# One more product per pair in a seven-product matmul stage, with its operands 0, 64 or 128 bytes apart

## The chip, the cores and the metric

The kernel runs on one core of a Trainium2 chip. The metric is the time of one execution on the device, in microseconds (us), lower being better. A time is the median of the runs shown; a profile is one further execution, and its own time is given beside it.

## The reference

One layer of an encoder over 512 tokens of 1024 channels, all in float32:

```python
h = rms_norm(x, norm1_g)
proj = h @ w_in                       # pooling, attention, recurrence, gates
...                                   # three branches, gated and summed, w_out, residual
h2 = rms_norm(x, norm2_g)
gu = h2 @ w_ffn_in                    # (512, 1024) @ (1024, 2 * 2816)
x = x + (silu(gu[..., :2816]) * gu[..., 2816:]) @ w_ffn_out
return rms_norm(x, final_norm_g)
```

The change lies in the line `gu = h2 @ w_ffn_in`.

## The kernel before

Products of float32 matrices are made from rounded parts: each operand is split into `hi` (rounded to the matmul's float32r form, a cast on ScalarE) and `lo` (the rest, a subtraction on VectorE), and a product is three matmuls into one PSUM bank: hi by hi, hi by lo and lo by hi. `whi` and `wlo` are the parts of weights, `shi` and `slo` those of sums of weights, `h_hi` and `h_lo` those of the transposed activations, `fhi` and `flo` those of sums of activations.

The hidden layer has 22 blocks of 128 gate columns and 22 of 128 up columns. Block 0 is computed plainly. Blocks 1 to 21 are pairs, one gate block and one up block each, of a two by two scheme with seven products in place of eight: the 1024 channels are halved, the 512 tokens are halved, and the products are of sums of halves. One product (`product`, helper `mm`, line 90) is 12 matmuls: three terms of 4 blocks of 128 channels, with 256 tokens (columns) streaming and 128 weight columns standing in the array. A pair is four bodies, `first` (products into `x` and `zy`), `second`, `third` (two each) and `fourth` (one), 84 matmuls in all. `first` uses part 0 of the pair, the split weights of one block (`whi`, 1024 elements per partition); `second` and `third` use parts 1 and 2 (`shi`, `slo`, from `sums`); `fourth` uses part 3 (`whi`, 512 elements).

TensorE works in the order in which the program is written. The other engines' instructions are placed by a scheduler that models the time, each engine working through its own queue in order. What comes between:

- The raw weights of a pair come by two DMAs from the SP queue into one of two `raw` buffers; the next transfer starts when the last reader of a buffer is done.
- Line 180 (ScalarE) and line 181 (VectorE) split parts 0 and 3 into `whi` and `wlo`, of which there are three buffers each; a cast waits until TensorE has read the old contents. Lines 258, 261 and 262 make `sums` on VectorE; lines 297 and 299 split them into `shi` and `slo`.
- Results are taken out of PSUM at lines 1123, 1134, 1136 and 1155 (ScalarE) and 1145, 1150 and 1156 (VectorE), the last of which writes the hidden block.

PSUM has three banks called `mm`, three called `rc` and two called `tp`. In the pairs `x` lies in an `mm` bank and `zy` in an `rc` bank. `tp` is used before the pairs for transposes and after them as the fourth accumulator of the output projection; during the pairs it is free.

Some places of tiles in the built program, in bytes from the start of a partition: the three `whi` buffers 35104, 39200 and 43296, `wlo` 47392, 51488 and 55584, the first norm's activations `hT` 69408 and 85792, `shi` 162080 and 166176, `slo` 170272 and 174368, all 32 past a multiple of 128. `h_hi` (61408), `h_lo` (77792), `fhi` (178656) and `flo` (195040) start 96 past one; `pad` lines of the program shift them. A block of 128 weight columns takes 512 bytes, one of 256 or 512 tokens 1024 or 2048, so that these remainders hold for every block.

Of the kernel before, what the change touches and what calls it, by code (L numbers as in the profile page):

```python
# [18 lines left out]
P = 128  # L19
# [57 lines left out]
def encoder_kernel(ctx: ExitStack, tc: tile.TileContext, x, norm1_g, w_in, pool_w, pool_scale,  # L77
# [11 lines left out]
    def mm(out_, lhsT, rhs, start, stop, chain=False):  # L89
        i = nc.tensor.matmul(out_, lhsT=lhsT, rhs=rhs, start=start, stop=stop, skip_group_check=chain)  # L90
        tc.keep_in_program_order(i)
        n = 1
        for d in rhs.shape[1:]:
            n *= d
        pipe.t += max(0.107, n * 0.0004167 + 0.002) if rhs.dtype == F32R else max(0.216, n * 0.001667 + 0.004)
# [18 lines left out]
    def bank(name, shape=(P, 512)):  # L114
        return psum.tile(list(shape), F32, name=name, bufs=2 if name == "tp" else 3)
# [148 lines left out]
    @contextmanager  # L264
    def behind(after):

        with ExitStack() as st:
            for i in after:
                st.enter_context(tc.issue_after(i))
            yield  # L270
# [45 lines left out]
    def product(ps, part, n, r, start):  # L316

        terms = [(part.hi, r[0]), (part.hi, r[1]), (part.lo, r[0])]
        for i, (w, m) in enumerate(terms):
            for k in range(KT // 2):  # L320
                mm(ps, w[:, n, k, :], m[:, k, :], start and i == 0 and k == 0,
                   i == 2 and k == KT // 2 - 1, True)
                if k % 2:
                    yield
# [147 lines left out]
    for b in range(NB):  # L472
# [3 lines left out]
        if b >= 1:  # L476
            c = OFF[("rq", "rf", "rb")[b - 1]]
# [583 lines left out]
    def ffn_pair_evac(j, pg, pu):  # L1061
        sl = FF["t"].tile([P, S], F32, name="silu")
        nc.scalar.activation(out=sl, in_=pg, func=AF.Silu)
        nc.vector.tensor_tensor(out=hid_of(j), in0=pu, in1=sl, op=ALU.mult)

    def hid_of(j):
        return FF["hid"][j // 8][:, j % 8, :]
# [3 lines left out]
    def hid_split(half, jp):  # L1071

        if (half, jp) in hid_parts:
            return
        early = half == 0 and jp < 2
        hi, lo = ((LAST["ws"] if early else FF["hs"]).tile([P, 2, S], F32R, name=n)
                  for n in (("shi", "slo") if early else ("hhi", "hlo")))
        j = 2 * jp
        view = FF["hid"][j // 8][:, j % 8:j % 8 + 2, :]
        nc.scalar.copy(out=hi, in_=view)  # L1080
        nc.vector.tensor_tensor(out=lo, in0=view, in1=hi.bitcast(F32), op=ALU.subtract)
        hid_parts[half, jp] = hi, lo
# [31 lines left out]
    def ffn_pair_bodies(j):  # L1114
        c = {}


        def first(part):
            f = FF["forms"]
            c["x"], c["zy"] = bank("mm")[:, 0:256], bank("rc")  # L1120
            c["u"] = FF["t"].tile([P, S], F32, name="u")
            yield from product(c["x"], part, 0, f.r11, True)
            nc.scalar.copy(out=c["u"][:, 0:256], in_=c["x"])
            yield from product(c["zy"][:, 0:256], part, 1, f.r21, True)

        def second(part):
            f = FF["forms"]
            y = c["y"] = c["zy"][:, 256:]
            if j == 2:
                with behind(FF["s12_2"]):  # L1130
                    ffn_pair_evac(0, *FF["first"])
            c["g"] = FF["t"].tile([P, S // 2], F32, name="g2")
            yield from product(c["x"], part, 1, f.n2, False)
            nc.scalar.copy(out=c["u"][:, 256:], in_=c["x"])
            yield from product(y, part, 0, f.n1, True)
            FF["y1"] = (nc.scalar.copy(out=c["g"], in_=y).ins,)

        def third(part):
            f = FF["forms"]
            if j == 1:  # L1140
                with behind(FF["forms_end"]):
                    pairs[2][1].chunk.add()
            c["sl"] = FF["t"].tile([P, S], F32, name="silu")
            yield from product(c["x"], part, 0, f.d, False)
            on_dve = nc.vector.tensor_tensor(out=c["g"], in0=c["x"], in1=c["g"], op=ALU.add).ins
            if j == 1:
                FF["g1"] = (on_dve,)
            nc.scalar.activation(out=c["sl"][:, 256:], in_=c["g"], func=AF.Silu, scale=-1.0)
            yield from product(c["y"], part, 1, f.r22, False)
            nc.vector.tensor_tensor(out=c["u"], in0=c["u"], in1=c["zy"], op=ALU.add)  # L1150

        def fourth(part):
            f = FF["forms"]
            yield from product(c["x"], part, 0, f.n4, False)
            nc.scalar.activation(out=c["sl"][:, 0:256], in_=c["x"], func=AF.Silu, scale=-1.0)
            nc.vector.tensor_tensor(out=hid_of(j), in0=c["sl"], in1=c["u"], op=ALU.mult)
            if j == FT - 1:
                for jp in range(2):
                    hid_split(0, jp)

        return first, second, third, fourth

    pair_bodies = {j: ffn_pair_bodies(j) for j in range(1, FT)}
    after = {1: (None, None, "forms_mid", "forms_mid"), 2: ("g1",) * 4, 3: ("s12_2",) * 4}
    pairs = {j: pair_parts(j, *ffn_cols(j), after.get(j, (None,) * 4)) for j in range(1, FT)}
# [71 lines left out]
    for half in range(2):  # L1237
        ps = list(row_parts(w_ffn_out[0], 0, FT, half * 512))
        n = NPC if half == 0 else NPC - TAIL
# [126 lines left out]
```

## Time and profile before

| | |
|---|---|
| runs | 912.06, 912.14 and 913.32 us; median 912.14 us |
| profiled execution | 912.07 us, of which the span of the profile is 910.3 us |
| TensorE matmuls, weight loads | 887.8 us busy (5353), 782.5 us (5353) |
| VectorE, ScalarE, GpSimd | 582.2, 420.9 and 62.0 us busy |
| DMA | 89.01 MB, on average 98 GB/s |

A line of the profile's timeline has the start and the length of a group of like instructions in us, the engine (PE is TensorE's matmuls, PEld its weight loads, DVE VectorE, ACT ScalarE, POOL GpSimd, SP the queue of the DMAs), the source line, the operation, "output<-inputs" by the program's names, the size, how many there are, and in brackets how long the engine had idled and what it had waited for. Matmuls overlap, so that the step from one start to the next, not the length, tells what one costs in a row of them.

### The profile page before, as it was taken

What the parts mean: (1) busy time and instruction counts of PE and PEld (TensorE: products, weight loads), DVE (VectorE), ACT (ScalarE), POOL (GpSimd) and SP (SyncE); (2) the same over time, 40 slices, a digit from 0 to 9 for tenths busy, and PEclk for the clock granted to TensorE, in tenths of its full rate; (3) what the DMA queues carried; (4) which work ended last, traced back from release to release, by engine and by line L of the source; (5) the groups of instructions that cost most, each with busy time, mean ns of one, the idle gap of its engine ahead of it and who ended that gap; (6) DMA issues with size and microseconds to landing.
All of it is one profiled execution on the core that took longest, in us unless ns stands there. A gap on an engine that the chain in (4) does not pass through costs nothing.

```text
span 910.3 us, 13173 instructions
## 1 busy us (share of the span) xinstructions
PE 887.8 (98%) x5353; PEld 782.5 (86%) x5353; DVE 582.2 (64%) x876; ACT 420.9 (46%) x652; POOL 62.0 (7%) x62
## 2 busy tenths in 40 slices
PE   6999999999999999999999999999999999999996
PEld 5977987887898888778888898999999999888885
DVE  5696553663867865654325554998888888644544
ACT  5544423433655674332233423765655556433433
POOL 2233311210000000000000000000000000000000
PEclk9999999999999999999999999999999999999998
DMA  8322030314033213522334250143433434323312
GB/s 249 101 69 70 3 92 24 115 47 154 27 107 96 81 60 109 183 90 94 95 118 154 96 163 0 47 134 100 138 95 111 122 94 137 118 70 106 113 37 93
DMA packets 106313, 89.01 MB, mean 98 GB/s; under 512 B 2686, under 2 KB 93324, under 8 KB 106124
## 3 DMA queue, kind: packets, MB, share of 16 engines
q1 hardware_dynamic: 105532, 86.59, 30.8%
q10 hardware_dynamic: 720, 1.57, 0.5%
q8 instruction: 42, 0.69, 0.3%
q14 instruction: 19, 0.16, 0.1%
HBM read 86.06 MB, written 2.10 MB: 97 GB/s over the span
## 4 chain that ended last, share of the span: by engine, by line
PE 87%; DVE 4%; issue 1%; ACT 0%; POOL 0%; POOLq 0%; DVEq 0%; ACTq 0%
PE mm L90 60%; PE rc L90 22%; PE tp L90 4%; PE tp L98 2%; DVE wlo L181 1%; DVE kq L755 1%; DVE pyr L765 0%; DVE l L848 0%; DVE pt L770 0%; DVE f L661 0%; ACT x L1209 0%; DVE og L791 0%; DVE slo L299 0%; POOL kq L758 0%; ACT silu L1197 0%
## 5 line engine op out<-in xcount | busy, mean ns | idle before, releaser
L181 DVE TENSOR_TENSOR wlo<-raw,whi 128x1024 fp32r<-128x1024 f32 (+1 forms) x146 | 170.2, 1169 | 165.5 <-PE mm L90 85.0
L180 ACT CAST whi<-raw 128x1024 fp32r<-128x1024 f32 (+1 forms) x146 | 143.7, 990 | 205.3 <-PE mm L90 122.1
L90 PE MATMUL mm<-hT_hi,whi 128*128 128x512 f32 (+1 forms) x440 | 110.6, 389 | 0.0
L90 PE MATMUL mm<-hT_hi,wlo 128*128 128x512 f32 (+1 forms) x440 | 108.3, 383 | 0.0
L90 PE MATMUL mm<-hT_lo,whi 128*128 128x512 f32 (+1 forms) x440 | 108.0, 382 | 0.0
L90 PEld LDWEIGHTS mm<-hT_hi,whi 128*128 128x128 f32 x440 | 79.2, 191 | 16.0 <-issue 1.9
L90 PEld LDWEIGHTS mm<-hT_lo,whi 128*128 128x128 f32 x440 | 79.2, 188 | 15.0
L90 PEld LDWEIGHTS mm<-hT_hi,wlo 128*128 128x128 f32 x440 | 78.8, 188 | 15.4 <-issue 1.0
L299 DVE TENSOR_TENSOR slo<-sums,shi 128x1024 fp32r<-128x1024 f32 x42 | 51.1, 1218 | 0.2 <-ACT shi L297 0.2
L297 ACT CAST shi<-sums 128x1024 fp32r<-128x1024 f32 x42 | 44.2, 1052 | 2.2 <-DVE sums L261 1.8
L758 POOL TENSOR_TENSOR kq<-kq,pyr 128x512 f32<-128x512 f32 x24 | 33.4, 1392 | 46.4 <-ACT kc L724 27.5
L90 PEld LDWEIGHTS rc<-kq,kc 128*128 128x128 f32 x224 | 29.7, 191 | 6.7 <-issue 2.4
L90 PE MATMUL rc<-kq,kc 128*128 128x128 f32 x224 | 32.1, 287 | 3.0 <-DVE kq L755 3.0
L755 DVE TENSOR_TENSOR kq<-kq,pyr 128x256 f32<-128x256 f32 x56 | 26.1, 507 | 13.1 <-PE rc L90 13.0
L724 ACT COPY kc<-kq 128x512 f32<-128x512 f32 x28 | 18.7, 668 | 30.1 <-POOL kq L758 21.3
L882 ACT ACTIVATE s<-s,mx 128x512 f32<-128x512 f32 x32 | 23.0, 720 | 16.2 <-DVE mx L880 16.0
L90 PE MATMUL mm<-fhi,slo 128*128 128x256 f32 x168 | 26.2, 278 | 0.5 <-DVE slo L299 0.5
L90 PE MATMUL mm<-y_hi,whi 128*128 128x512 f32 x96 | 26.4, 393 | 0.0
L90 PE MATMUL mm<-y_lo,whi 128*128 128x512 f32 x96 | 26.2, 392 | 0.0
L90 PE MATMUL mm<-fhi,shi 128*128 128x256 f32 x168 | 26.0, 277 | 0.1
L90 PE MATMUL mm<-flo,shi 128*128 128x256 f32 x168 | 25.9, 276 | 0.0
L90 PE MATMUL mm<-y_hi,wlo 128*128 128x512 f32 x96 | 25.9, 390 | 0.0
(253 smaller groups left out, 1809.8 us busy)
## 6 DMA issues: line engine op xcount, KB each, us to landing
raw<-in_w_ffn_in_dram SPq DMA_DIRECT2D x44, 512.0 KB, 5.2
raw<-in_w_in_dram SPq DMA_DIRECT2D x18, 1024.0 KB, 5.2
raw<-in_w_in_dram SPq DMA_DIRECT2D x24, 512.0 KB, 4.2
raw<-in_w_ffn_out_dram SPq DMA_DIRECT2D x10, 1024.0 KB, 5.1
raw<-in_w_out_dram SPq DMA_DIRECT2D x4, 1024.0 KB, 5.3
xin<-in_x_dram SPq DMA_DIRECT2D x4, 512.0 KB, 9.3
raw<-in_w_up_rec_dram SPq DMA_DIRECT2D x2, 1024.0 KB, 7.7
x<-in_x_dram SPq DMA_DIRECT2D x1, 2048.0 KB
```

What stands on the lines that cost most here:

```text
L90: i = nc.tensor.matmul(out_, lhsT=lhsT, rhs=rhs, start=start, stop=stop, skip_group_check=chain)
L98: tc.keep_in_program_order(nc.tensor.transpose(out_, in_, idn))
L180: nc.scalar.copy(out=hi, in_=view)
L181: nc.vector.tensor_tensor(out=lo, in0=view, in1=hi.bitcast(F32), op=ALU.subtract)
L297: nc.scalar.copy(out=hi, in_=view)
L299: on_dve = nc.vector.tensor_tensor(out=lo, in0=view, in1=hi.bitcast(F32), op=ALU.subtract).ins
L724: nc.scalar.copy(out=strided(kc, 0, [[2 * n, S // (2 * n)], [n, 2], [1, n]]), in_=strided(kq, 2 * S, [[2 * n, S // (2 * n)], [S + n, 2], [ ...
L755: nc.vector.tensor_tensor(out=xv, in0=xv, in1=tv, op=ALU.mult)
L758: (nc.gpsimd if n < 128 else nc.vector).tensor_tensor(out=xv, in0=xv, in1=tv, op=ALU.mult)
L882: nc.scalar.activation(out=s, in_=s, func=AF.Exp, scale=-1.0, bias=mx[:, c:c + 1], accum_out=zz[:, i, c:c + 1])
```

## The change

In `first`, from the third pair on (j = 3 to 21), one more matmul follows the two products. Its standing weights are the first 128 columns of the pair's own `whi`, its stream is 256 or 512 columns of the same `whi`, from element 0, 16 or 32 on (0, 64 or 128 bytes), in turn with j. It writes a `tp` bank, as a group of its own, and nothing reads the result.

```diff
             yield from product(c["zy"][:, 0:256], part, 1, f.r21, True)
 
+
+            if j >= 3:
+                n, skip = ((512, 0), (256, 0), (256, 16), (256, 32), (512, 16))[j % 5]
+                w = part.hi.rearrange("p n k c -> p (n k c)")
+                mm(bank("tp")[:, 0:n], w[:, 0:P], w[:, skip:skip + n], True, True)
+
         def second(part):
```

The program gains six lines, so that line 1145 of before is 1151 of after, and so on. On TensorE the new matmul stands between the second product of `first` and the first product of `second`. Before, in the fifth pair:

```order
L90 MATMUL rc<-h_hi,whi 128x256 x4
L90 MATMUL rc<-h_lo,whi 128x256 x4
L90 MATMUL rc<-h_hi,wlo 128x256 x4
L90 MATMUL mm<-fhi,shi 128x256 x4
L90 MATMUL mm<-flo,shi 128x256 x4
```

Now:

```order
L90 MATMUL rc<-h_hi,whi 128x256 x4
L90 MATMUL rc<-h_lo,whi 128x256 x4
L90 MATMUL rc<-h_hi,wlo 128x256 x4
L90 MATMUL tp<-whi 128x512
L90 MATMUL mm<-fhi,shi 128x256 x4
L90 MATMUL mm<-flo,shi 128x256 x4
```

One row of one matmul has come in; the rest of TensorE's order is as it was. With the new matmul the `whi` tile of `first` has a later last reader. The cast into its buffer waits for that, and the scheduler has answered on VectorE, in 16 of the pairs. Before, in one of them (`g` and `hid` carry buffer numbers here):

```order
L258 TENSOR_TENSOR sums<-raw 128x2x512
L1156 TENSOR_TENSOR hid_4880<-silu,u 128x512
L181 TENSOR_TENSOR wlo<-raw,whi 128x512
L261 TENSOR_TENSOR sums<-sums,raw 128x512
L262 TENSOR_TENSOR sums<-sums,raw 128x512
L1145 TENSOR_TENSOR g_5509<-mm,g_5509 128x256
L299 TENSOR_TENSOR slo<-sums,shi 128x1024
```

Now:

```order
L258 TENSOR_TENSOR sums<-raw 128x2x512
L1162 TENSOR_TENSOR hid_4880<-silu,u 128x512
L261 TENSOR_TENSOR sums<-sums,raw 128x512
L181 TENSOR_TENSOR wlo<-raw,whi 128x512
L262 TENSOR_TENSOR sums<-sums,raw 128x512
L1151 TENSOR_TENSOR g_5517<-mm,g_5517 128x256
L299 TENSOR_TENSOR slo<-sums,shi 128x1024
```

The subtraction that makes the 512-element `wlo` and one of the additions for `sums` have changed places. ScalarE, GpSimd and the DMA queue keep their order.

## The prediction

> **What bounds the kernel now.** I read the page first (busy times, the 40 slices, the chain that ended last), then the table by stages around the changed stage, then the timeline of one pair, matmul by matmul. The page says which engine to look at:
>
> ```profile
> span 910.3 us, 13173 instructions
> ...
> PE 887.8 (98%) x5353; PEld 782.5 (86%) x5353; DVE 582.2 (64%) x876; ACT 420.9 (46%) x652; POOL 62.0 (7%) x62
> ...
> PE   6999999999999999999999999999999999999996
> ...
> PE 87%; DVE 4%; issue 1%; ACT 0%; POOL 0%; POOLq 0%; DVEq 0%; ACTq 0%
> ```
>
> TensorE is busy in every slice and carries 87% of the chain. Busy time alone proves little, since matmuls overlap, so the stage has to be looked at for gaps. The next table has the stretch before the third pair, then pairs 3 to 21 (19 pairs, in which all the added products stand), then the output projection:
>
> ```profile
> core 0: us, PE busy (x) PEld busy (x) DVE busy (x) ACT busy (x) POOL busy (x), PEclk, DMA share, GB/s
> 590.00:601.80 11.80, 11.21 (x94) 10.62 (x93) 11.53 (x16) 6.58 (x12) 0.00 (x0) 1.00 0.48 132
> 601.80:782.50 180.70, 180.70 (x1597) 180.70 (x1596) 154.38 (x190) 105.48 (x174) 0.00 (x0) 1.00 0.42 117
> 782.50:903.10 120.60, 120.22 (x544) 99.88 (x542) 59.87 (x73) 47.09 (x63) 1.60 (x3) 1.00 0.24 83
> ```
>
> In the middle row TensorE is busy for 180.70 of 180.70 us at a granted clock of 1.00, and so is its weight load; VectorE has 26 us to spare (180.70 - 154.38), ScalarE 75, and the DMA engines are 42% busy. Behind it TensorE lacks only 0.38 us of 120.60. So nothing in the stage or after it could take up a delay of TensorE: what is added to its stream there comes out at the end, one for one. The price of a matmul is then not its duration but the step from one start to the next. One pair, in the timeline of TensorE:
>
> ```profile
> 639.91 0.62 PE L90 MATMUL mm<-h_hi,whi 128*128 128x256 f32 x4
> ...
> 642.18 0.62 PE L90 MATMUL rc<-h_hi,wlo 128*128 128x256 f32 x4
> 642.63 0.62 PE L90 MATMUL mm<-fhi,shi 128*128 128x256 f32 x4
> ...
> 649.43 0.62 PE L90 MATMUL mm<-h_hi,whi 128*128 128x256 f32 x4
> ```
>
> From 639.91 to 649.43 one pair's 84 matmuls take 9.52 us, 113.3 ns each. The added product goes in at 642.63, between `rc<-h_hi,wlo` (the end of `first`) and `mm<-fhi,shi` (the start of `second`).
>
> **The change, part by part.** Since j % 5 picks the form for j = 3 to 21, there are 19 products: 4 of 512 columns at skip 0 (j = 5, 10, 15, 20), 4 of 512 at 64 bytes (4, 9, 14, 19), 4 of 256 at 0 (6, 11, 16, 21), 3 of 256 at 64 (7, 12, 17), 4 of 256 at 128 (3, 8, 13, 18). Each brings its own weight load of 128 columns.
>
> What does the distance do? The trace has the same 256-column matmul at two steps. In the load rows of the pair above, the weights of a matmul begin to load one step before it starts, beside the stream of its predecessor:
>
> ```profile
> 642.18 0.62 PE L90 MATMUL rc<-h_hi,wlo 128*128 128x256 f32 x4
> 642.52 0.53 PEld L90 LDWEIGHTS mm<-fhi,shi 128*128 128x128 f32 x4
> ```
>
> So the distance that can matter is that between what streams and the weights that load beside it. In the built program `h_hi`, `h_lo`, `fhi`, `flo` start 96 bytes past a multiple of 128, and `whi`, `wlo`, `shi`, `slo` 32 past: 64 bytes apart, modulo 128, and 113.3 ns. In the value projection of attention both operands (`hT`, `whi`) start 32 past, that is 0 apart:
>
> ```profile
> 264.55 1.11 PE L90 MATMUL mm<-whi,hT_lo 128*128 128x256 f32 x8
> 265.50 1.12 PE L90 MATMUL mm<-wlo,hT_hi 128*128 128x256 f32 x8
> 266.46 1.12 PE L90 MATMUL mm<-whi,hT_hi 128*128 128x256 f32 x8
> ```
>
> 8 matmuls in 0.96 us (265.50 to 266.46): 120 ns, 6.7 more. The Trainium skill ("TensorE: Matmul & The Clock Gate", step-by-step part) says the opposite: the moving operand and the weight load have independent read ports, and loading the next weights takes no bandwidth from the running matmul. By that rule every 256-column product would cost 113.3 ns whatever the distance, and the sum below would be 0.05 us less; these rows speak against it, though the distance is not the only thing that differs between the two places.
>
> Of the added product, the stream is `whi` plus skip and the weights beside it are the next product's `shi`. Both start 32 past, so skip 0 and 128 are 0 apart, skip 64 is 64 apart. Eight products of 256 columns then cost 120 ns (0.960 us), three 113.3 (0.340 us). Reading the distance as that between the added product's own two operands, as the change's words have it, gives the same classes.
>
> For 512 columns at 0 apart the output projection has rows, after its first three:
>
> ```profile
> 782.71 0.39 PE L90 MATMUL rc<-whi,shi 128*128 128x512 f32 x1
> ...
> 783.40 0.39 PE L90 MATMUL rc<-whi,shi 128*128 128x512 f32 x1
> ...
> 784.08 0.39 PE L90 MATMUL rc<-whi,shi 128*128 128x512 f32 x1
> ```
>
> Three in 0.68 us (783.40 to 784.08), 226.7 ns. For 512 columns 64 apart the only rows lie in a stretch that is slow for another reason (below):
>
> ```profile
> 578.14 2.02 PE L90 MATMUL rc<-h_hi,whi 128*128 128x512 f32 x8
> 580.00 2.03 PE L90 MATMUL rc<-h_lo,whi 128*128 128x512 f32 x8
> 583.74 0.63 PE L90 MATMUL mm<-fhi,shi 128*128 128x256 f32 x4
> 584.21 0.63 PE L90 MATMUL mm<-flo,shi 128*128 128x256 f32 x4
> ```
>
> That is 232.5 ns (1.86 us over 8) as the upper bound; the lower is 226.7 less the 6.7 that the 256-column rows gain, 220. I take 226.7, between them and from undisturbed rows. Eight of 512: 1.813 us. Sum at a steady pace: 0.960 + 0.340 + 1.813 = 3.11 us; with the bounds for the four, 3.09 to 3.14.
>
> A single product of another shape also disturbs the pace around it. At the switch from 256 to 512 columns the three from 782.71 to 783.40 took 0.69 us, 10 ns over the steady pace. The switch back from 512 to 256 columns, 64 bytes apart, stands ahead of the changed stage:
>
> ```profile
> 568.34 0.70 PE L90 MATMUL mm<-wlo,m_hi 128*128 128x512 f32 x2
> 568.88 0.62 PE L90 MATMUL mm<-h_hi,whi 128*128 128x256 f32 x4
> 569.34 0.62 PE L90 MATMUL mm<-h_lo,whi 128*128 128x256 f32 x4
> 569.80 0.62 PE L90 MATMUL mm<-h_hi,wlo 128*128 128x256 f32 x4
> 570.25 0.62 PE L90 MATMUL rc<-h_hi,whi 128*128 128x256 f32 x4
> ```
>
> The first four (568.88 to 569.34) took 0.46 instead of 0.453 us, 7 ns more; by 569.80 the usual step is back. So I add 10 + 7 ns for each of 512 and half of the 7 for each of 256: 8 x 17 + 11 x 3.5 = 0.17 us (bounds 0 and, with 17 for all, 0.32). Total 3.3 us, with bounds from 3.1 to 3.5.
>
> Waits. From the third on, each added product waits for the product two before it, because `tp` has two buffers; that was 168 matmuls or 19 us earlier, so the wait is met. It is also the last reader of the first `whi` tile, which the cast of the 512-element `whi` on ScalarE waits for. On it hang, in their queues:
>
> ```profile
> 642.42 0.63 ACT L180 CAST whi<-raw 128x512 fp32r<-128x512 f32 x1 [0.58 <-PE rc L90]
> 644.19 0.37 ACT L1134 COPY u<-mm 128x256 f32<-128x256 f32 x1 [1.14 <-PE mm L90]
> ...
> 643.62 0.68 DVE L181 TENSOR_TENSOR wlo<-raw,whi 128x512 fp32r<-128x512 f32 x1
> 644.23 0.68 DVE L261 TENSOR_TENSOR sums<-sums,raw 128x512 f32<-128x512 f32 x1
> ...
> 646.98 0.42 DVE L1145 TENSOR_TENSOR g<-mm,g 128x256 f32<-128x256 f32 x1 [1.34 <-PE mm L90]
> ```
>
> The release moves from 642.42 to about the added product's end (642.63 plus a duration of 0.28 to 0.39, so 643.0), 0.6 us later. The cast then ends near 643.7, in front of the copy at 644.19, which idles 1.14 us for TensorE. On VectorE the scheduler lets line 261 go first in 16 pairs; the same work is done in another order and ends before the 1.34 us of idle time in front of `g`. I cost both at nothing; if that cover were gone, the `g` add and the `silu` behind it would come late, and the fourth product's evacuation with them. The pair itself grows by 0.12 to 0.23 us, which gives both engines more room, not less.
>
> So 912.07 us (the profiled execution, 1.8 us of it around the span) becomes 915.4. The median of the runs shown is 0.07 above that execution, and one of three was 1.25 above; I predict 915.4.
>
> **The rivals.** *Every disturbance sticks.* From 583.74 to 584.21 four matmuls took 117.5 ns each at the distance where the stage runs at 113.3, a slow pace that set in behind a gap and stayed over more than one product. If each added product put the stream into it until the next, 84 x 4.2 ns x 19 = 6.7 us would come on top: 922; in half the pairs, 918.7. Against it: behind the 512 columns at 568.34 the usual step was back within eight matmuls, and the stage holds it through 133 products of changing operands. Chance 0.09.
>
> *Each added product empties the pipeline*, so that it costs its duration (0.39 us for 512 columns as in the rows at 782.71, and for 256 the 0.62 us of four less three steps, 0.28) plus the step: 11 x 0.28 + 8 x 0.39 = 6.2 us more, 921.6 us; if only the part of the duration over the step is lost, 163 ns x 19 = 3.1 us, 918.4. The Trainium skill (same page, "Single matmul latency") has such a cost for a matmul that stands alone. Against it: every product of the stage starts and ends a group of its own in another bank, at no cost. Chance 0.04.
>
> *Not slower: TensorE's stream is not the pace-maker.* If the weights' transfers or VectorE set 9.52 us per pair, the added products would fall into waiting time and the time would stay at 912.1. That decides from the point at which another engine needs more than about 9.7 us per pair; VectorE has 154.38 us in 19 pairs, 8.1 each, and TensorE shows no idle time at all in the stage. Chance 0.03. *The products don't run*, because nothing reads their result: 912.1 too; but the built program has 19 more matmuls. Chance 0.01. A gain could only come from the stall rows ahead of the stage, which the change does not touch: 0.01.
>
> **How the numbers follow.** The forecast has 0.82: 915.2 to 915.6 by its bounds, and up to 916.9 with the 1.25 us by which one of the three runs lay above the others. The range 914.8 to 917.0 holds that and the smallest part of the sticking case. Less than 0.2% (1.8 us) can't be told from no change here, so only times over 914.0 count as slower: the forecast, the first two rivals: 0.95. Same 0.04, faster 0.01.
>
> **What would show it.** Nineteen `tp<-whi` matmuls, 8 of 512 and 11 of 256 columns. Pairs 9.63 or 9.75 us apart instead of 9.52. `mm<-fhi,shi` behind the added product 0.12 or 0.23 us later than now against `rc<-h_hi,wlo`, and 113.3 ns from there on. No idle time of TensorE in the stage, the output projection 3.3 us later and otherwise unchanged, the idle time in front of `g` still there. I would be wrong if matmuls behind an added product kept 117 ns, if its step were nearer 0.4 than 0.23 us, or if the distance classes came out alike or reversed.

## The result: 921.24 us, 9.1 us slower, and the profile after

| | before | after |
|---|---|---|
| runs | 912.06, 912.14, 913.32 us | 920.11, 921.24, 921.31 us |
| median | 912.14 us | 921.24 us |
| ratio | | 1.0092, 95% interval 1.0069 to 1.0115 |
| profiled execution | 912.07 us (span 910.3) | 921.31 us (span 919.5), one of the three runs |

The busy times on the page after, with each engine's share of the span and its number of instructions:

```profile
PE 896.9 (98%) x5372; PEld 791.6 (86%) x5372; DVE 580.0 (63%) x876; ACT 420.7 (46%) x652; POOL 62.8 (7%) x62
```

Nineteen matmuls and nineteen weight loads have come in, and TensorE's busy time has grown by 9.1 us (896.9 - 887.8): 0.48 us for each. The table by stages, as shown of before, with the granted clock in the third column from the right:

```profile
core 0: us, PE busy (x) PEld busy (x) DVE busy (x) ACT busy (x) POOL busy (x), PEclk, DMA share, GB/s
602.60:791.90 189.30, 189.30 (x1617) 188.96 (x1616) 153.27 (x190) 105.61 (x173) 0.00 (x0) 1.00 0.40 112
791.94:912.50 120.56, 119.99 (x542) 99.67 (x540) 59.80 (x73) 46.93 (x64) 1.65 (x3) 1.00 0.25 83
```

and the same stretch behind the stage in the kernel before, in the same columns:

```profile
782.71:903.27 120.56, 120.00 (x542) 99.67 (x540) 59.83 (x73) 46.94 (x64) 1.65 (x3) 1.00 0.24 83
```

The output projection takes 120.56 us in both. The granted clock is 1.00, and TensorE is never idle in pairs 3 to 21, as before; yet that stage now takes 189.31 us (602.63 to 791.94) instead of 180.88 (601.83 to 782.71). So it is neither a wait nor the clock: the matmuls themselves follow each other at another pace. The timeline of TensorE after shows it at two added products of 512 columns, both 64 bytes apart (j = 4 and j = 9):

```profile
614.20 0.62 PE L90 MATMUL rc<-h_lo,whi 128*128 128x256 f32 x4
614.65 0.62 PE L90 MATMUL rc<-h_hi,wlo 128*128 128x256 f32 x4
615.11 0.40 PE L90 MATMUL tp<-whi 128*128 128x512 f32 x1
615.34 0.64 PE L90 MATMUL mm<-fhi,shi 128*128 128x256 f32 x4
615.81 0.63 PE L90 MATMUL mm<-flo,shi 128*128 128x256 f32 x4
...
664.92 0.63 PE L90 MATMUL rc<-h_hi,wlo 128*128 128x256 f32 x4
665.39 0.40 PE L90 MATMUL tp<-whi 128*128 128x512 f32 x1
665.62 0.62 PE L90 MATMUL mm<-fhi,shi 128*128 128x256 f32 x4
666.08 0.62 PE L90 MATMUL mm<-flo,shi 128*128 128x256 f32 x4
666.53 0.62 PE L90 MATMUL mm<-fhi,slo 128*128 128x256 f32 x4
```

Read the steps, not the lengths. Four matmuls take 0.45 us ahead of the first one (614.20 to 614.65) and 0.47 behind it (615.34 to 615.81); at the second it is the other way round, 0.47 ahead (664.92 to 665.39) and soon 0.45 behind (666.08 to 666.53). The same instruction, with the same distance, slows the stream once and speeds it up once, and what it leaves lasts through the 84 matmuls up to the next added product. I call them the short pace, 113.33 ns a matmul, and the long pace, 117.78 ns (over the 72 steps behind the first twelve of a pair; the expectations below have 117.75). Even the records' lengths tell them apart. The matmuls of one product term in one pair, eight of them in two blocks, grouped by tile, with least, median and greatest ns; first from the pair of j = 3 (short), then from that of j = 5 (long):

```profile
L90 PE MATMUL mm<-fhi,slo x8: 276/276/276, 606.5 to 609.6; 128*128 128x256 f32 x8
...
L90 PE MATMUL mm<-fhi,slo x8: 281/281/281, 626.4 to 629.6; 128*128 128x256 f32 x8
```

Each of the first is 276 ns, each of the others 281. Behind their added product, five pairs (j = 3, 9, 12, 13, 19) run at the short pace and fourteen at the long one.

The third pair was already entered at the long pace. The last wait ahead of it is the same in both profiles, a wait for VectorE's `slo`; the timeline after, and then before:

```profile
599.23 0.74 PE L90 MATMUL mm<-fhi,slo 128*128 128x256 f32 x4 [0.46 <-DVE slo L299]
599.80 0.63 PE L90 MATMUL rc<-h_hi,shi 128*128 128x256 f32 x4
600.27 0.40 PE L90 MATMUL rc<-h_lo,shi 128*128 128x256 f32 x2
```

```profile
598.53 0.74 PE L90 MATMUL mm<-fhi,slo 128*128 128x256 f32 x4 [0.47 <-DVE slo L299]
599.11 0.62 PE L90 MATMUL rc<-h_hi,shi 128*128 128x256 f32 x4
599.56 0.62 PE L90 MATMUL rc<-h_lo,shi 128*128 128x256 f32 x4
```

After 0.46 us of waiting the stream went on at 0.47 us for four, after 0.47 us at 0.45. No instruction of the change stands ahead of this place, and VectorE's first exchange comes 25 us behind it.

The 9.24 us between the two profiled executions are then: 3.16 us for the steps of the 19 products themselves (1.85 for the eight of 512 columns, 1.31 for the eleven of 256); 5.12 us for 1152 matmuls at the long pace (13 pairs of 84 and the last pair's 60, by 4.44 ns); 0.2 us for the stretch from the wait at 599.23 to the first added product, also at the long pace; 0.7 us that the execution was already late at that wait (599.23 against 598.53), far ahead of the change; and less than 0.1 us of single uneven steps.

### The profile page after: what moved, and what is told of

It is laid out like the page before. It is cut to its first block, busy times and chain, and to the rows that moved or that the text cites. A ratio compares the mean times of both kernels' runs of the same rounds, so it can differ in the third digit from the quotient of the medians.

```text
span 919.5 us, 13193 instructions
## 1 busy us (share of the span) xinstructions
PE 896.9 (98%) x5372; PEld 791.6 (86%) x5372; DVE 580.0 (63%) x876; ACT 420.7 (46%) x652; POOL 62.8 (7%) x62
## 5 line engine op out<-in xcount | busy, mean ns | idle before, releaser
L1151 DVE TENSOR_TENSOR g<-mm,g 128x256 f32<-128x256 f32 x21 | 8.9, 424 | 31.6 <-PE mm L90 31.6
```

## The experiments

Three theories stood against each other at first. *The pace sticks* (A): an added product can put TensorE's stream into the other pace, and it stays there until something else disturbs it. *A price per product* (B): each added product itself costs 9.1/19 = 0.48 us. *The late release* (C): `whi` comes free later, ScalarE and VectorE work in another order, and the matmuls behind suffer for it. All edits replace the two lines that choose `n` and `skip`, unless shown otherwise.

**One product alone (e1_one_512).**

```diff
-            if j >= 3:
-                n, skip = ((512, 0), ...)[j % 5]
+            if j == 4:
+                n, skip = 512, 0
```

> One added product in place of nineteen: 512 columns at skip 0, in the fourth pair only. VectorE's order is that of the kernel before. Theory A (the products are cheap, but a product of another shape puts the stream of 256-column matmuls into a second pace of 117.75 ns instead of 113.33, which lasts until something disturbs it again): nothing comes after it, so all of the remaining 17 pairs run slow, 0.23 us for the product plus about 1490 matmuls x 4.42 ns = 6.6 us, about 918.9 us. Theory B (each added product itself costs 9.1/19 = 0.48 us, by an emptied pipeline or a wait): 912.6. Theory C (the later release of whi and VectorE's other order slow the stage): 912.4, since only one pair has the later release.

919.68 us, the median of 10 runs (919.01 to 921.29), against 912.72 for the kernel before on that chip; ratio 1.0061 (1.0034 to 1.0087). One matmul costs 7 us. The timeline of TensorE from it on, and, grouped by tile, all the `mm<-fhi,slo` from there to the end of the stage:

```profile
616.02 0.39 PE L90 MATMUL tp<-whi 128*128 128x512 f32 x1
616.26 0.63 PE L90 MATMUL mm<-fhi,shi 128*128 128x256 f32 x4
```

```profile
L90 PE MATMUL mm<-fhi,slo x144: 281/281/281, 617.2 to 788.6; 128*128 128x256 f32 x144
```

Its own step is 232 ns (0.23 of the 7 us; 616.02 to 616.26 by the rounded rows), so the theory of a price per product falls. Behind it all 144 of these matmuls have the 281 ns of the long pace, least and greatest alike: 18 pairs, 171 us, with no other added product, no late release in any later pair, and VectorE's order as before. The pace sticks, and nothing in the stage brings it back.

**All alike: e2_all_256_64, e3_all_512_0, e4_all_256_0.** The line of `n, skip` becomes `256, 16`, `512, 0` or `256, 0` for every j from 3 on. In all three the release is late in every pair, and VectorE's order is the changed one (e3 has one more exchange on VectorE and one on ScalarE, at 610 us).

> Nineteen added products, all of 256 columns and 64 bytes apart, the shape and distance of the stage's own matmuls. whi is released as late as in the changed kernel and VectorE's order is changed in the same 16 pairs. Theory A: nothing breaks the rhythm, so a stream that enters at 113.33 ns keeps it: 19 x 0.113 = 2.15 us, 914.3 (up to 7 us more only if the stream enters the third pair in the slow pace and is not brought back). Theory B (a price per added product): about 921. Theory C (other engines): about 2.2 us for the products and the same 5 to 6 us on top, 920.

> Nineteen added products, all of 512 columns at skip 0. Theory A: in the changed kernel every one of the four products of this form left the slow pace behind it, whatever the pace ahead of it, so all pairs from the third on are slow: 19 x 0.229 = 4.4 us plus 18 x 84 x 4.42 ns + 60 x 4.42 ns = 6.9 us, about 923.4. Theory B: 512 columns cost more than 256, 912.1 + 19 x 0.53 = 922, without a slower pace of the matmuls between. Theory C: 912.1 + 4.4 + 5.5 = 922.

> Nineteen added products, all of 256 columns at skip 0 (0 bytes apart). In the changed kernel the four products of this form met a slow stream each time and left it slow; what they do to a fast one was not seen. Theory A gives two times: 19 x 0.120 = 2.3 us, 914.4, if the fast pace survives them, and 914.4 + 6.9 = 921.3 if the first one breaks it. Theory B: 912.1 + 19 x 0.42 = 920, with 113.33 ns between them. Theory C: 920, with the pace between them at 113.33 or 117.75 whichever form is added.

| | median us (runs) | ratio to before | pace ahead of a product and behind it |
|---|---|---|---|
| e2: 256 columns, 64 bytes | 918.35 (10) | 1.0051 (1.003 to 1.0072) | turns at every product, 10 of 19 pairs long |
| e3: 512 columns, 0 bytes | 924.00 (6) | 1.0108 (1.0075 to 1.0141) | short at the first, long behind all 19 |
| e4: 256 columns, 0 bytes | 915.46 (10) | 1.0014 (0.9989 to 1.0038) | long ahead of the first, short behind all 19 |

Two stretches of e2, each from behind one added product to the next, in the columns of the table by stages:

```profile
605.04:614.93 9.89, 9.89 (x86) 9.89 (x85) 9.12 (x12) 5.58 (x9) 0.00 (x0) 1.00 0.58 161
615.05:624.59 9.54, 9.54 (x87) 9.54 (x85) 8.33 (x11) 5.49 (x9) 0.00 (x0) 1.00 0.47 126
```

The same 84 matmuls take 9.89 and then 9.54 us, with TensorE busy throughout, and so on in turn. And e4 behind the product of j = 6, in the timeline:

```profile
634.79 0.64 PE L90 MATMUL mm<-fhi,shi 128*128 128x256 f32 x4
635.26 0.62 PE L90 MATMUL mm<-flo,shi 128*128 128x256 f32 x4
635.71 0.62 PE L90 MATMUL mm<-fhi,slo 128*128 128x256 f32 x4
```

Four take 0.47 us and then 0.45 again. e4 has the late release and the changed order in every pair and runs at the short pace, so the theory of the late release falls. There a product costs 0.14 us in all: its step of 119 ns, and 118, 124 and 119 ns for three of the matmuls behind. e2 was expected at 914.3 because I held 64 bytes for the stage's own distance; it behaved as another distance, which led to the next three.

**Is the period 256 bytes? (e5_all_256_192).** In the built program the stage's streams start 224 bytes past a multiple of 256 and its weights 32 past: 192 apart. By 128 that is the same as 64, by 256 it isn't. The line becomes `n, skip = 256, 48`, that is 192 bytes.

> Nineteen added products of 256 columns, the stream starting 192 bytes behind the weights. The stage's own matmuls stand 192 bytes apart if the distance counts modulo 256 and not 128 (the stream 224 past a multiple of 256, the weights 32 past one). Theory A with a period of 256 bytes: the added product is then like its neighbours, step 113.33 ns, no jolt, the pace that enters the third pair stays: 912.7 + 2.15 = 914.9, or 914.9 + 7.0 = 922 if it enters slow. Theory A with a period of 128 bytes: 192 is the same as 64, the pace changes over in every pair as with 64, and the time is that of the products at 64 bytes, 918.4. Theory C (whi released later, VectorE's other order): 918, as with 64 bytes.

914.57 us (10 runs, seven at 913.83 to 915.07, three at 922.09 to 922.39); ratio 1.0022 (0.9981 to 1.0062). In the timeline:

```profile
614.44 0.28 PE L90 MATMUL tp<-whi 128*128 128x256 f32 x1
614.56 0.62 PE L90 MATMUL mm<-fhi,shi 128*128 128x256 f32 x4
615.01 0.62 PE L90 MATMUL mm<-flo,shi 128*128 128x256 f32 x4
```

The product takes one step, 113.3 ns, like the four behind it (0.45 us), and the stream holds the short pace through all nineteen. At 64 bytes it turned the pace every time, at 192 in this execution never. Only `skip` differs between e2, e4 and e5, so neither the `tp` bank nor a group of its own is what costs. The three long runs were not profiled; 922 is what the expectation has for a stream that enters at the long pace.

**The step at each distance (e6_sweep_256, e7_sweep_512).** One execution each: 32 matmuls in a row in place of one, at another distance in each pair, 0 to 288 bytes by 16.

```diff
+                n, skip = 256, 4 * (j - 3)          # e7: 512
...
+                ps = bank("tp")
+                for i in range(32):
+                    mm(ps[:, 0:n], w[:, 0:P], w[:, skip:skip + n], i == 0, i == 31)
```

> A measurement: in each pair from the third on, 32 added matmuls of 256 columns in a row with the same operands, at distances of 0, 16, 32 up to 288 bytes, one distance per pair. Theory A (the step depends on the distance between the stream and the weights that load beside it): each run of 32 settles at a step of its own, 120 ns at 0 and at 256, 113.3 ns at 192, repeating with a period of 256 bytes, with 64 either 113.3 (period 128) or another value. Theory B (the distance is nothing, a product that is foreign to the stream costs more): the 32 settle at one and the same step at all distances. The time is of no interest: about 912.7 + 19 x 32 x 0.117 = 984 us.

> The same with 512 columns: 32 added matmuls in a row per pair, at distances of 0, 16 up to 288 bytes. Theory A: 226.7 ns at 0 and 256, and some 231 to 236 at 64 or 192, where the start of the feed-forward stage has these steps; the distances with the lowest step need not be those of 256 columns. Theory B: one step for all distances. The time is of no interest: about 912.7 + 19 x 32 x 0.229 = 1052 us.

987.69 and 1057.50 us. Rows of e6 at 0 and 192 bytes, each with the row behind it, whose start ends the 32 steps:

```profile
606.76 3.98 PE L90 MATMUL tp<-whi 128*128 128x256 f32 x32
610.58 0.64 PE L90 MATMUL mm<-fhi,shi 128*128 128x256 f32 x4
...
767.66 3.79 PE L90 MATMUL tp<-whi 128*128 128x256 f32 x32
771.29 0.50 PE L90 MATMUL mm<-fhi,shi 128*128 128x256 f32 x3
```

32 steps take 3.82 and 3.63 us. The mean of the last 20 steps, in ns:

| bytes apart | 0 | 16 | 32 | 48 | 64 | 80 | 96 | 112 | 128 | 144 | 160 | 176 | 192 | 208 | 224 | 240 | 256 | 272 | 288 |
|---|---|---|---|---|---|---|---|---|---|---|---|---|---|---|---|---|---|---|---|
| 256 columns | 120.0 | 116.7 | 116.7 | 118.4 | 117.8 | 120.0 | 120.0 | 113.3 | 118.7 | 118.7 | 117.3 | 119.0 | 113.4 | 119.5 | 118.2 | 116.9 | 120.0 | 116.7 | 116.7 |
| 512 columns | 226.7 | 231.7 | 233.4 | 233.3 | 229.0 | 231.2 | 233.4 | 231.1 | 233.4 | 233.3 | 234.4 | 231.0 | 233.4 | 234.7 | 233.4 | 236.7 | 226.7 | 231.7 | 233.3 |

The row repeats from 256 on (0, 16 and 32 have their values again to 0.1 ns) and not from 128 on. With nothing but the start of the stream moved, a step goes from 113.3 to 120.0 ns for 256 columns and from 226.7 to 236.7 for 512. By itself that can't tell the distance from the stream's own address, since the weights start 32 bytes past a multiple of 256 throughout. The trace of before can. At 522.22 us `whi` streams, 32 past, as at 0 bytes in the sweep and as in the value projection at 264.55; but the weights beside it, `m_hi` and `m_lo`, start 96 past in the built program (179808 and 196192), so that the distance is 192:

```profile
522.22 0.87 PE L90 MATMUL mm<-whi,m_hi 128*128 128x256 f32 x6
...
527.87 0.87 PE L90 MATMUL mm<-wlo,m_hi 128*128 128x256 f32 x6
...
530.77 1.07 PE L90 MATMUL mm<-whi,m_hi 128*128 128x256 f32 x8
...
543.46 1.07 PE L90 MATMUL mm<-wlo,m_hi 128*128 128x256 f32 x8
```

48 matmuls take 5.65 us up to 527.87 (117.7 ns each), and 112 take 12.69 from 530.77 on (113.3 ns): the two paces of 192 bytes, and not the 120 ns that the same stream has beside `hT`. So the distance counts. The Trainium skill ("TensorE: Matmul & The Clock Gate", step-by-step part) has independent read ports for the stream and the weight load, so that a load takes nothing from the running matmul; these rows contradict it, by up to 6%. For 192 bytes the table has only the short pace; the long one at that distance has the mean, 117.8 ns, that 64 bytes has.

**Kick and cure (e8_kick_cure, e9_cure_only).** If a single product starts the long pace, a longer row at distance 0 might end it, as the single product at 605.45 did after the change (256 columns, 128 bytes). e8 gives j = 4 one product of 512 columns and j = 5 ten of 256, e9 j = 3 the ten alone, all at skip 0:

```diff
-            if j >= 3:
-                n, skip = ((512, 0), ...)[j % 5]
+            for n in {4: [512], 5: [256] * 10}.get(j, []):     # e9: {3: [256] * 10}
```

> The product of the run with a single one (512 columns at skip 0, fourth pair), and in the fifth pair ten products of 256 columns at skip 0. Ten are enough for the step to settle at 120 ns, as in the measured row of 32, behind which the stage ran at 113.33. Theory A (what the single product costs is the pace that lasts behind it): 117.75 ns for the 84 matmuls of the fourth pair, 0.37 us, then 113.33 again: 912.5 + 0.23 + 0.37 + 1.2 = 914.3, less than with the single product alone (919.7) although ten more are added. If the cost is in the products or on other engines: 919.7 + 1.2 = 920.9.

> The ten products of 256 columns at skip 0 alone, in the third pair. Some runs of the kernel before took 919.0 to 920.8 us where the others took 911.8 to 914.4. Theory A: those are runs whose stream came into the third pair at 117.75 ns and kept it for 19 pairs, 1596 x 4.42 ns = 7.1 us. The ten products end that, so that all runs take 912.5 + 1.2 = 913.7 and none 919 or more. If the longer runs have another cause, one in five of these should still take about 921.

e8: 915.36 us (10 runs, 914.45 to 916.42), ratio 1.0007 (0.9981 to 1.0033). e9: 914.88 us (10 runs, 913.96 to 916.29), ratio 0.9997 (0.9966 to 1.0028). Neither interval shows a difference from before, which has long runs of its own on that chip (4 of 19). That e9 has none fits theory A, but at one run in five ten would miss them by chance about once in ten times; e8 is the stronger test, since its product at j = 4 alone left all ten runs of e1 at 919 us or more. The timeline of e8 around the ten:

```profile
623.47 0.63 PE L90 MATMUL rc<-h_hi,wlo 128*128 128x256 f32 x4
623.94 2.17 PE L90 MATMUL tp<-whi 128*128 128x256 f32 x10
625.95 0.62 PE L90 MATMUL mm<-fhi,shi 128*128 128x256 f32 x4
626.41 0.62 PE L90 MATMUL mm<-flo,shi 128*128 128x256 f32 x4
626.86 0.62 PE L90 MATMUL mm<-fhi,slo 128*128 128x256 f32 x4
```

The single 512 had set the long pace (0.47 us for four, 623.47 to 623.94), the ten ended it (0.45, 626.41 to 626.86), and the 1400 matmuls behind them keep the short one. Where e1 lost 7 us, e8 loses 2.4 (915.36 against 913.01). That it isn't the 914.3 expected is a price of its own: the ten take 2.01 us (623.94 to 625.95), not 1.2, because each asks for a `tp` bank, there are two, and the third and later ones wait for the product two before; they follow at 221 ns.

**Four in a row, four one by one (e10_cure_four, e11_four_singles).** The ten without the wait for a bank: four into one bank at j = 3, or one each at j = 3 to 6; all 256 columns at 0 bytes.

```diff
+            if j == 3:                                # e10
...
+                ps = bank("tp")
+                for i in range(4):
+                    mm(ps[:, 0:256], w[:, 0:P], w[:, 0:256], i == 0, i == 3)
...
+            if 3 <= j <= 6:                           # e11
+                n, skip = 256, 0
```

> Four matmuls of 256 columns at skip 0, as one group in one tp bank, in the third pair alone. In the run with ten, eight of them stood 221 ns apart, not 120, since each asked for a tp buffer and there are two; in one group they should stand at about 120, 0.5 us in all. Theory A: a stream that comes in fast leaves at 113.33 as behind the single products at skip 0. One that comes in slow leaves fast if four are enough: all runs at 912.6 + 0.5 = 913.1 and none at 919 or more, where about one in five runs of the kernel before is. If four are not enough, some runs lie at 920.

> Single products of 256 columns at skip 0 in the third to the sixth pair, four in all, 84 matmuls apart, and nothing after. Theory A: a fast stream survives each of them (in the run with nineteen it did, at about 0.14 us each), and a slow one gets four chances at four different places of its rhythm to come back. All runs at 912.7 + 0.6 = 913.3, none at 919 or more, and the mean below that of the kernel before, whose runs lie at 912 to 914 four times in five and at 919 to 921 once in five. If a slow stream is not brought back, one run in five lies at 920; in four matmuls without a gap the pace ended slow each time, so that what counts would be the exact place, not the form.

e10: 920.18 us in the median of 11 runs, all between 919.52 and 921.04; ratio 1.0069 (1.0049 to 1.0089). In the timeline it is entered at the short pace and left at the long one:

```profile
604.91 0.62 PE L90 MATMUL rc<-h_hi,wlo 128*128 128x256 f32 x4
605.36 0.63 PE L90 MATMUL tp<-whi 128*128 128x256 f32 x4
605.83 0.64 PE L90 MATMUL mm<-fhi,shi 128*128 128x256 f32 x4
606.30 0.64 PE L90 MATMUL mm<-flo,shi 128*128 128x256 f32 x4
```

So the cure was the kick: one product at distance 0 kept the short pace in e4, four in a row ended it. My expectation, 913.1, had the form deciding; the number decides as well.

e11: 913.37 us, the median of 13 runs, of which twelve lie at 912.61 to 914.20 and one, the profiled one, at 921.82; ratio 0.9982 (0.9957 to 1.0008), which is not that of the medians (913.37 against 912.86) and shows no difference. That one was entered at the long pace behind the wait at 600.6, and four single products didn't end it:

```profile
606.35 0.63 PE L90 MATMUL rc<-h_hi,wlo 128*128 128x256 f32 x4
606.82 0.28 PE L90 MATMUL tp<-whi 128*128 128x256 f32 x1
606.94 0.64 PE L90 MATMUL mm<-fhi,shi 128*128 128x256 f32 x4
607.41 0.64 PE L90 MATMUL mm<-flo,shi 128*128 128x256 f32 x4
...
782.54 0.64 PE L90 MATMUL mm<-h_hi,whi 128*128 128x256 f32 x4
783.01 0.64 PE L90 MATMUL mm<-h_lo,whi 128*128 128x256 f32 x4
```

0.47 us for four ahead, behind, and still at 782.54, at the end of the stage. In e4 the same product at the same place in the program, also met at the long pace, did end it (at 605.68 us: 117.8 ns a matmul ahead of it, 113.3 behind). e11 shows what an execution of 8 us more looks like: its stream enters the stage at the long pace and keeps it. Its short runs were not profiled, but e2 and e4, which have one and the same program up to that place, entered at different paces.

The kernel before does that too. Over the chips of these experiments it ran 92 times: 72 runs at 911.8 to 914.4 us and 20 at 919.0 to 921.2, none between. 19 pairs of 84 matmuls by 4.44 ns are 7.1 us, about the distance of the groups. No long run of before was profiled, so for it this is arithmetic; for e11 the trace shows it. No version has a median below that of before, so none is offered as better. Kernels with products at 0 bytes in every pair or ten in a row (e4, e8, e9) had no long run among 30, which might be worth a change where the worst run counts.

## Why the prediction was wrong

**Right in the sum: the products' own steps.** The sum at a steady pace was 3.11 us; measured, 3.16. The eight of 512 columns took 226 to 234 ns (1.85 us against 1.81), the eleven of 256 113 to 122 ns (1.31 against 1.30). That the 256s agree so well is luck: the classes did not come out. Those at 0 bytes took 113 or 122 ns (117.5 in the mean, 120 predicted), those at 64 bytes 120.3 (113.3 predicted), those at 128 bytes 118.8 (120 predicted), and the errors cancel. The prediction had named reversed classes as a sign of being wrong.

**Right: one for one.** TensorE has no idle time in the stage, and the output projection behind it keeps its 120.56 us; the delay comes out at the end whole.

**Right: the waits cost nothing.** The cast of the 512-element `whi`, released later now, and the copy behind it, in ScalarE's timeline after:

```profile
645.73 0.62 ACT L180 CAST whi<-raw 128x512 fp32r<-128x512 f32 x1 [1.20 <-PE tp L90]
...
647.10 0.37 ACT L1140 COPY u<-mm 128x256 f32<-128x256 f32 x1 [0.75 <-PE mm L90]
```

The releaser is now `tp`, and the copy still idles 0.75 us for TensorE. VectorE's `g` keeps its idle time in the page after, 31.6 us over 21 additions, against 22.8 in the kernel before (the last two columns: busy us and mean ns, idle before them and its releaser):

```profile
L1151 DVE TENSOR_TENSOR g<-mm,g 128x256 f32<-128x256 f32 x21 | 8.9, 424 | 31.6 <-PE mm L90 31.6
```

e4 shows the same from the other side: all of these waits, and the short pace.

**The step that failed: the disturbance, 8 x 17 + 11 x 3.5 ns = 0.17 us.** It took a disturbance for something that fades within eight matmuls. It measured 5.1 us in the pairs, 30 times as much, because the pace that a product leaves lasts until the next one: the matmuls behind an added product kept 117.78 ns in fourteen pairs, the first sign of being wrong that the prediction names. The prediction had the row that says so, the four from 583.74 on at 117.5 ns, and gave the case that follows from it ("every disturbance sticks", 922) a chance of 0.09; it argued against it from the return at 568.88, and from the stage holding its pace through 133 products. The first was one outcome of several, as 615.34 and 665.62 show; the second doesn't speak against sticking, but for it: a stream that keeps its pace through 133 products will keep the other one too, as e1's 18 pairs did. The trace of before had both, in the rows from 522.22 us shown above, and the prediction did not use them. The size that the rival gave was nearly right: of the 6.7 us worked out for all pairs, 5.1 came, since five pairs of nineteen fell to the short pace.

**Also wrong: distances modulo 128.** The classes repeat with 256 bytes, so skip 64 is not the stage's own distance. For the products' own steps this changes hundredths of a microsecond; but I took the 64-byte products for harmless on its account, and e2, with nothing else, loses 5.6 us (918.35 against 912.72) where e5, at the stage's 192 bytes, loses the 2.0 of its own steps.

**Not considered: the pace at the entry.** The range went by three runs within 1.3 us. With 20 of 92 runs of before near 920, one kernel's single execution can lie 7 to 8 us off whatever the change does.

The other rivals fell: no product cost its duration (a step behind 512 columns is 226 to 234 ns, not 390 and more), and the products run.

## What to carry to other kernels

In a stage that TensorE fills without a gap, price an added matmul by the steps of the hundreds behind it, not by its own: compare the starts of like rows just ahead, just behind and at the end of the stage. Where a trace holds two paces of the same instruction at the same clock and the same distance, take the slower one for something that can come back and stay, and look at single runs for two groups before trusting a median of three. Where addresses can be chosen, measure the step at several distances between stream and weights over a whole 256 bytes.

## What the runs showed of the hardware that I had not expected

- Back-to-back matmuls of one shape, at granted clock 1.00, took 113.3 to 120.0 ns (256 columns) and 226.7 to 236.7 ns (512 columns) with the distance between what streams and the weights that load beside it, modulo 256 bytes (e6, e7: distances 0 to 288 bytes, the stream moved; for moved weights there are only the rows of before at 522.22 us).
- At 192 bytes one stream has two lasting paces, 113.33 and 117.78 ns. One other matmul can turn it either way (e1, e4), and it stays for 1500 matmuls (e1).
- Which way it turns depends on more than shape, distance and the pace ahead: one product of 256 columns at 0 bytes, met at the long pace at the same place, ended it in e4 and not in e11, and four in a row did to the short pace what one did not (e10, e4). It looks like a matter of where in the rhythm of stream and loads the foreign step falls; no run here shows that rhythm itself, and why there are two paces, why 256 bytes, and what decides the entry behind the last wait before the third pair stay open.
